# One decoder step on one core: the sampled tokens' state space steps move beside the recurrence heads, the gate norm's sums go through memory, the forget gate becomes a tangent

## The chip, the core and the metric

The kernel runs on one core of one Trainium2 chip. The metric is the device time in microseconds (us) of one execution. Its engines are PE (matrix products, with PEld for loading the stationary operand), DVE (vector), ACT (activations and copies), POOL (a second, slower vector engine) and SP (which here only issues transfers). Each engine works through its own list of instructions in order, so an instruction that waits holds up all that stand behind it on that engine.

## The reference, cut to what matters

One hybrid decoder layer is computed for a prompt of 1024 tokens and for 8 sampled tokens (one new token each, with their own stored states), which the kernel keeps side by side as 1032 columns.

```python
proj = rmsnorm(x, w['norm1_w']) @ w['w_in']
q_r, f_r, i_r, g_r, z, xbc_r, dt_r = jnp.split(proj, splits, axis=-1)
f = lb + (1.0 - lb) * sigmoid(f_r);  k = 1.0 - f;  q = silu(q_r)        # 8 heads, gated recurrence
o_a = rmsnorm(hgrn2_mix(q, k, i_r, log(f), S_h)) * silu(g_r)
xs, Bm, Cm = split(silu(causal_dwconv(xbc_r, buf_s)))                     # state space mixer, 2 groups
y, S_s_new = ssd_scan(X * dt, A * dt, Bh, Ch, S_s)
y = (y + D * X) * silu(z)
y = rmsnorm(y.reshape(Bsz, L, 2, 512)) * ssm_norm_w                       # norm over a group's 512 channels
x = x + concat(o_a, y) @ w['w_out']
x = x + (silu(causal_dwconv(gate)) * val) @ w['w_down']                   # gate, val = norm(x) @ w_up
```

For a sampled token the state space mixer is a single step: the stored state (64 x 128 per head) is scaled by its decay, a product of input and B is added, the new state is written out, and its product with C, summed over 128, is the output.

## The kernel before, in words

Channels lie on the 128 partitions and tokens along the free axis. A float32 product is made of three reduced ones (high and low parts of both operands), so a projection of 128 channels over 344 columns takes 24 matrix products; three such column chunks make a **job** of 72 steps (in_job). Jobs stand in one list: the state space inputs x0 to x7 with B and C, then the gate jobs z0 to z3, head 0's four jobs (f0, q0, v0, sg0), z4 to z7, and the jobs of heads 1 to 7, then the output projection. PE's list is written by hand: drive() runs a job's steps and, spread among them, the pieces of a second stream: the chunks of the state space scan (ssd_front, ssd_back), first for group 0 over the x jobs up to x7, then for group 1 over z0 to v0, and then head(h) over the jobs of head h + 1. after(n, work) puts a piece of work n steps later. On the other engines, and in SP's list of transfers, the framework orders the instructions by a plan of its own, at compile time.

What the change touches:

- **ssm_decode(g, i)** (L625): the sampled tokens' step for 128 channels, eight in all. For each half (4 tokens) it loads B and C of the tokens spread over the partitions (Bb, Cb) and the stored state (Sd); ACT scales the state (L638, 4 instructions), DVE multiplies B by the input (L639) and adds (L640), the state goes out, POOL multiplies by C (L642), DVE sums (L643). The steps of group 0 begin with jobs x5, x7, z0 and z1, beside the two scans; those of group 1 with z4 to z7.
- The scan: ssd_back needs the state S of the chunk before (DVE, L580) for its product yo, and ssd_front's xdt (DVE, L554) for yd. The convolution of a job (conv_tail, L347) puts three DVE instructions over 1056 columns into the same list.
- **ssm_gate(g)** (L653): each z job multiplies a tile of the scan's output by silu(z), and sums squares into gacc. For each of three chunks rstd() then sums over the partitions with a product by ones (ms), 344 columns wide on all 128 partitions, makes the reciprocal root in three DVE instructions (rstd_of, L649 to L651), and after the last one tail() scales four tiles (L694) and writes them to mix_d, with the sampled tokens' 8 columns in the same rows.
- **head_in(h)** (L806): f through Sigmoid (L818), q and sg through Silu. ACT keeps one table of functions at a time and loads another by an ACT_TABLE_LOAD.
- **head(h)** (L829): products named a (from k, v, f, q, scaled level by level on DVE, L872 and L873), od (the sampled tokens, from the state tiles Sh), ktp (transposes, copied to kt by ACT, L951), kv, the chain of states SS on DVE (L962, L964), and o. Sd and Sh use the same two buffers; Bb, Cb and vb the same four.

Of the kernel before, what the change touches and what calls it, by code (L numbers as in the profile page):

```python
# [50 lines left out]
def hybrid_layer(  # L51
# [37 lines left out]
    def bank(s, tag="mx"):  # L89
        return psmx.tile([P, 512], F32, tag=tag, bufs=NBANK[tag], name=nm(s))  # L90

    def mm(out, lhsT, rhs, start=True, stop=True):
        PE.matmul(out, lhsT, rhs, start=start, stop=stop)  # L93
# [55 lines left out]
    def col(name, i=0):  # L149
        c = vlay[name] + i  # L150
        return vcol[:, c:c + 1]
# [77 lines left out]
    def after(n, work):  # L229

        later.append([n, work])
# [123 lines left out]
    def xbc_evict(j, ext, c, cs, ps):  # L355
        e = min(cs.stop, T)
        A.copy(ext[:, 3 + cs.start:3 + e], ps[:, :e - cs.start])
        if c == 2:
            V.tensor_copy(ext[:, 3 + T:3 + T + 32].rearrange("p (b r) -> p b r", r=4)[:, :, 3:4],
                          ps[:, T - cs.start:].unsqueeze(2))  # L360
            V.tensor_copy(last11[:, j, :], ps[:, CH - 11:])

    def xbc_close(j, ext):
# [166 lines left out]
    def ssd_front(g, c, parts):  # L530
        tsl = slice(c * P, (c + 1) * P)
        hc = c * 16 + g * 8
        lm = []
        for q in range(2):
            csb = half("csb")
            csb3 = csb.rearrange("p (h l) -> p h l", l=P)
            h0 = hc + q * 4
            fetch(csb, cs_d[0, h0:h0 + 4, :].rearrange("h l -> (h l)").unsqueeze(0).to_broadcast([P, 512]))

            for h in range(4):  # L540
                A.activation(csb3[:, h, :], csb3[:, h, :], AF.Relu, scale=-1.0, bias=cst[:, h0 + h:h0 + h + 1])
            A.activation(csb, csb, AF.Exp, scale=-1.0)
            lm.append(csb3)
        bg = bank("bg")
        PE.transpose(bg[:, 0:P], BT[g][:, tsl], ident)
        mm(bg[:, P:2 * P], BT[g][:, tsl], CT[g][:, tsl])
        bt = small.tile([P, 2, P], F32, tag="bt", bufs=2, name=nm("bt"))
        A.copy(bt[:, 0, :], bg[:, 0:P])
        V.tensor_tensor(bt[:, 1, :], bg[:, P:2 * P], tri, op=ALU.mult)
        xp = bank("xp")  # L550
        for i in range(4):
            PE.transpose(xp[:, i * P:(i + 1) * P], Xg[g][i][:, tsl], ident)
        xdt, xde = half("xdt"), half("xde")
        V.tensor_tensor(h64(xdt), h64(xp), b64(dt, hc), op=ALU.mult)  # L554
# [70 lines left out]
    def ssm_decode(g, i):  # L625
        j = g * 4 + i
        xdd = small.tile([P, 2, ND], F32, tag="xdd", name=nm("xdd"))
        xdec = Xg[g][i][:, T:NT]
        V.tensor_tensor(xdd[:, 0, :], xdec, ddb[:, 0, j, :], op=ALU.mult)
        for b0 in (0, 4):  # L630
            bs = slice(b0, b0 + 4)
            Bb, Cb = tl("d", "Bb")[:, :512], tl("d", "Cb")[:, :512]
            for t_, r in ((Bb, 2 * g), (Cb, 2 * g + 1)):
                fetch(t_, bc_d[r, bs].rearrange("b n -> (b n)").unsqueeze(0).to_broadcast([P, 512]))
            Sd = tl("ld", "Sd")
            fetch(d4(Sd), state_ssm[0, bs, 2 * j:2 * j + 2].rearrange("b h p n -> (h p) b n"))
            for b in range(4):
                A.activation(d4(Sd)[:, b, :], d4(Sd)[:, b, :], AF.Copy, scale=ddb[:, 1, j, b0 + b:b0 + b + 1])  # L638
            V.tensor_tensor(d4(Bb), d4(Bb), cb(xdd[:, 0, bs]), op=ALU.mult)  # L639
            V.tensor_tensor(Sd, Sd, Bb, op=ALU.add)  # L640
            SP.dma_start(ssm_sample[0, bs, 2 * j:2 * j + 2].rearrange("b h p n -> (h p) b n"), d4(Sd))
            G.tensor_tensor(Cb, Sd, Cb, op=ALU.mult)  # L642
            V.tensor_reduce(xdd[:, 1, bs], d4(Cb), axis=mybir.AxisListType.X, op=ALU.add)  # L643
        V.scalar_tensor_tensor(xdec, xdec, d_bc[:, j:j + 1], xdd[:, 1, :], op0=ALU.mult, op1=ALU.add)

    def rstd_of(dst, tmp, ps, n):

        A.activation(dst, ps, AF.Abs_reciprocal_sqrt, bias=epsc, scale=1.0 / n)
        V.scalar_tensor_tensor(tmp, ps, n * EPS, dst, op0=ALU.add, op1=ALU.mult)  # L649
        V.scalar_tensor_tensor(tmp, tmp, -0.5 / n, dst, op0=ALU.mult, op1=ALU.mult)  # L650
        V.scalar_tensor_tensor(dst, tmp, 1.5, dst, op0=ALU.add, op1=ALU.mult)  # L651

    def ssm_gate(g):  # L653
        acc = []

        def z_job(i):
            j = g * 4 + i

            def begin():
                if i == 0:  # L660
                    acc.append(tl("g", "gacc"))
                if g:
                    ssm_decode(1, i)
                elif i < 2:
                    ssm_decode(0, i + 2)

            def evict(c, cs, ps):
                Y = Xg[g][i][:, cs]
                sz = tl("z", "sz")[:, :CH]
                A.activation(sz, ps, AF.Silu)  # L670
                V.tensor_tensor(Y, Y, sz, op=ALU.mult)
                if i == 0:
                    A.activation(acc[0][:, cs], Y, AF.Square)
                else:
                    A.activation(sz, Y, AF.Square)
                    (V if g or i == 3 else G).tensor_tensor(acc[0][:, cs], acc[0][:, cs], sz, op=ALU.add)
                if i == 3:
                    after(36 + 14 * g, lambda: rstd(c))
            in_job(f"z{j}", OFF_Z + j * P, evict, begin=begin)

        def rstd(c):
            cs = chunks[c]
            ps = bank("ms", "nx")
            mm(ps[:, :CH], ones, acc[0][:, cs])
            rstd_of(acc[0][:, cs], tl("z", "nt")[:, :CH], ps[:, :CH], 512)

            if c == NCH - 1:
                tail()

        def tail():  # L690
            for i in range(4):
                j = g * 4 + i
                Y = Xg[g][i][:, :NT]
                V.scalar_tensor_tensor(Y, Y, col("sn", j), acc[0][:, :NT], op0=ALU.mult, op1=ALU.mult)  # L694
                SP.dma_start(mix_d[8 + j], Y)

        for i in range(4):
            z_job(i)
# [35 lines left out]


    lbt = const.tile([P, 4, 8], F32, name="lbt")
    lo0, lo1 = vlay["lb"], vlay["lb"] + 8
    V.tensor_tensor(lbt[:, 0, :], vcol[:, lo0:lo0 + 8], vcol[:, lo1:lo1 + 8], op=ALU.max)
    V.tensor_tensor(lbt[:, 1, :], vcol[:, lo0:lo0 + 8], lbt[:, 0, :], op=ALU.subtract)
# [3 lines left out]
    V.reciprocal(lbt[:, 3, :], lbt[:, 3, :])  # L743
    V.tensor_tensor(lbt[:, 0, :], lbt[:, 1, :], lbt[:, 3, :], op=ALU.mult)
    V.tensor_scalar(lbt[:, 1, :], lbt[:, 0, :], -1.0, 1.0, op0=ALU.mult, op1=ALU.add)

    eye8 = const.tile([P, ND, ND], F32, name="eye8")
    G.memset(eye8, 1.0)
# [57 lines left out]
    def head_in(h):  # L806
        t = {}

        def f_end():
            f, k = t["f"], tl("big", "k")  # L810
            A.activation(f[:, :NT], f[:, :NT], AF.Identity, bias=lbt[:, 0, h:h + 1], scale=lbt[:, 1, h:h + 1])
            V.tensor_scalar(k[:, :NT], f[:, :NT], -1.0, 1.0, op0=ALU.mult, op1=ALU.add)
            t["k"] = k

        for n, off, func in (("f", OFF_F, AF.Sigmoid), ("q", OFF_Q, AF.Silu), ("v", OFF_I, AF.Copy),
                             ("sg", OFF_G, AF.Silu)):
            def evict(c, cs, ps, n=n, func=func):
                A.activation(t[n][:, cs], ps, func)  # L818
# [687 lines left out]
```

## Time and profile before

| | |
|---|---|
| median of 3 runs | 1765.32 us (1763.92 to 1766.82) |
| the profiled execution | 1763.89 us, its span 1762.2 us |
| PE busy | 1713.2 us, 97% of the span |
| DVE, ACT, POOL busy | 1105.4, 812.3, 482.0 us (63%, 46%, 27%) |
| granted PE clock, whole run | 0.994 |

PE is the engine to watch: what the others do matters where PE waits for them. A wait is shown as idle time before an instruction, with the engine and line that released it. PEclk is the clock that PE was granted in a stretch, 1.00 being full. Matrix products are pipelined: one lists as 0.32 us but the next starts 0.16 us later, so costs on PE are read from start to start.

### The profile page before, as it was taken

Reading aid. Unit: us, or ns where it says so; the run is one execution under the profiler, and the core shown is the slowest. Engines: PE = TensorE matmul, PEld = TensorE weight load, DVE = VectorE, ACT = ScalarE, POOL = GpSimd, SP = SyncE. Lnnn points to the kernel's source line nnn. Section 1 sums busy time; section 2 is a strip of 40 time slices with the busy share of each in tenths; the row PEclk is TensorE's granted clock in tenths of the full one; section 3 lists DMA queues with packets and bytes.
Section 4 is the critical chain, followed back from the end, with each engine's and each line's share of the span. In section 5 each row is a group of like instructions: output and inputs, shape, how many; then the busy total and the mean of one; then the engine's idle time right before and its main releaser. Section 6 shows DMA issues by size and latency. Waiting matters only on the chain. (4 is left out here: it accounts for less than half of the span.)

```text
span 1762.2 us, 38558 instructions
## 1 busy us (share of the span) xinstructions
PE 1713.2 (97%) x16111; PEld 1662.8 (94%) x16111; DVE 1105.4 (63%) x1988; ACT 812.3 (46%) x1450; POOL 482.0 (27%) x485
## 2 busy tenths in 40 slices
PE   7999899999999999999899999999999999999998
PEld 6999799998999999999799989999999999999997
DVE  6668966575554554466636688776667777445545
ACT  7577698454544454454423374334333434111114
POOL 2103332120110110112220355666666664000002
PEclk9999999999999999999899999999999999999999
DMA  5355744643321332234336742222222226422312
GB/s 166 68 147 155 189 117 136 179 139 105 88 89 51 98 87 80 69 115 143 110 113 212 245 127 73 73 85 85 85 73 73 80 78 217 152 85 78 98 61 97
DMA packets 249828, 199.17 MB, mean 113 GB/s; under 512 B 47212, under 2 KB 220822, under 8 KB 249638
## 3 DMA queue, kind: packets, MB, share of 16 engines
q1 hardware_dynamic: 249366, 196.61, 36.8%
q8 instruction: 126, 2.06, 0.5%
q14 instruction: 48, 0.39, 0.1%
q0 software_dynamic: 288, 0.10, 0.0%
HBM read 154.11 MB, written 46.94 MB: 114 GB/s over the span
## 5 line engine op out<-in xcount | busy, mean ns | idle before, releaser
L93 PE MATMUL mm<-hh,wh 128*128 128x344 f32 x1248 | 405.9, 326 | 2.0 <-issue 1.2
L93 PE MATMUL mm<-hl,wh 128*128 128x344 f32 x1248 | 405.5, 325 | 0.0
L93 PE MATMUL mm<-hh,wl 128*128 128x344 f32 x1248 | 402.4, 323 | 0.0
L93 PEld LDWEIGHTS mm<-hh,wh 128*128 128x128 f32 x1248 | 235.4, 189 | 6.5 <-issue 3.9
L93 PEld LDWEIGHTS mm<-hl,wh 128*128 128x128 f32 x1248 | 235.4, 189 | 4.5 <-issue 3.3
L93 PEld LDWEIGHTS mm<-hh,wl 128*128 128x128 f32 x1248 | 235.7, 189 | 1.8 <-issue 1.4
L190 ACT CAST wh<-ws 128x1024 fp32r<-128x1024 f32 x96 | 100.6, 1047 | 254.1 <-PE dn L93 135.0
L93 PE MATMUL ub<-uh,wh 128*128 128x258 f32 x704 | 199.3, 283 | 3.1 <-DVE fext L1319 2.7
L93 PE MATMUL ub<-ul,wh 128*128 128x258 f32 x704 | 199.0, 283 | 0.0
L93 PE MATMUL ub<-uh,wl 128*128 128x258 f32 x704 | 198.7, 282 | 0.0
L93 PE MATMUL dn<-ah,wh 128*128 128x256 f32 (+1 forms) x640 | 181.1, 283 | 2.0 <-DVE x L1436 2.0
L93 PE MATMUL dn<-al,wh 128*128 128x256 f32 (+1 forms) x640 | 180.6, 282 | 0.0
L93 PE MATMUL dn<-ah,wl 128*128 128x256 f32 (+1 forms) x640 | 180.1, 281 | 0.0
L192 DVE TENSOR_TENSOR wl<-ws,wh 128x1024 fp32r<-128x1024 f32 x88 | 108.7, 1235 | 75.7 <-ACT wh L190 68.6
L93 PE MATMUL mm<-mh,wh 128*128 128x258 f32 x512 | 148.2, 289 | 4.1 <-ACT x L1064 2.8
L93 PE MATMUL ua<-uh,wh 128*128 128x258 f32 x528 | 149.6, 283 | 1.3 <-DVE val L1331 1.3
L93 PE MATMUL ua<-ul,wh 128*128 128x258 f32 x528 | 149.3, 283 | 0.0
L93 PE MATMUL ua<-uh,wl 128*128 128x258 f32 x528 | 148.4, 281 | 0.0
L93 PE MATMUL mm<-ml,wh 128*128 128x258 f32 x512 | 146.9, 287 | 0.8 <-DVE ml L1024 0.8
L93 PE MATMUL mm<-mh,wl 128*128 128x258 f32 x512 | 146.5, 286 | 0.0
L93 PEld LDWEIGHTS ub<-uh,wh 128*128 128x128 f32 x704 | 132.9, 189 | 3.8 <-DVE fext L1319 2.9
L1269 DVE TENSOR_TENSOR wl<-wt,wh 128x512 fp32r<-128x512 f32 x88 | 89.6, 1037 | 74.2 <-ACT wh L1268 73.9
(351 smaller groups left out, 4037.2 us busy)
## 6 DMA issues: line engine op xcount, KB each, us to landing
ws<-in_w_in_dram SPq DMA_DIRECT2D x52, 512.0 KB
ws<-in_w_up_dram SPq DMA_DIRECT2D x44, 512.0 KB
ws<-in_w_out_dram SPq DMA_DIRECT2D x24, 512.0 KB
act_d<-val SPq DMA_DIRECT2D x22, 516.0 KB
al<-act_d SPq DMA_DIRECT2D x22, 516.0 KB
ws<-in_w_down_dram SPq DMA_DIRECT2D x22, 512.0 KB
ml<-mix_d SPq DMA_DIRECT2D x48, 172.0 KB
csb<-cs_d SPq DMA_DIRECT2D x32, 256.0 KB
```

Source lines behind the costliest of these rows:

```text
L93: PE.matmul(out, lhsT, rhs, start=start, stop=stop)
L190: A.copy(wh[:, :n], ws[:, :n])
L192: V.tensor_tensor(wl[:, :n], ws[:, :n], wh[:, :n].bitcast(F32), op=ALU.subtract)
L1269: V.tensor_tensor(lo[:, cs], sums[name], hi[:, cs].bitcast(F32), op=ALU.subtract)
```

## The change

- The eight ssm_decode steps leave the jobs x5, x7, z0, z1 and z4 to z7. They begin with jobs v and sg of heads 1 to 4, two to a head, so in the scan's stead they run beside head(0) to head(3). Their inputs and outputs move from the scan's tiles to a small tile of their own (xdk).
- After the fourth step of a group, decode_gate and decode_norm gate and normalise these 8 columns by themselves, with one small product by ones (dgs), and write them to mix_d.
- ssm_gate leaves the sampled columns out. rstd() runs once for a group: four products with 32 columns of ones put the sums of 1024 tokens on four strips of 32 partitions (256 columns each), one root over 256 columns follows, the result goes to memory (gr_d) and, 36 steps later, is read back spread over all partitions; 20 steps after that tail() scales the four tiles, 6 steps apart.
- f becomes Tanh of half the value, with the constants changed to match, since sigmoid(x) = 0.5 + 0.5 tanh(x / 2). Tanh is in the table that Silu is in.
- In ssd_front the second half's Relu comes ahead of both Exp. Head 0's k takes a buffer of another kind ("e").

```diff
         A.activation(acc[:, :T], acc[:, :T], AF.Silu)
-        A.activation(acc[:, T:NT], acc[:, T + 3:T + 32:4], AF.Silu)
+        A.activation(xdk[:, j, :] if j < 8 else acc[:, T:NT], acc[:, T + 3:T + 32:4], AF.Silu)
...
             ext.append(xbc_open())
-            if j in (5, 7):
-                ssm_decode(0, (5, 7).index(j))
...
             for h in range(4):
-                A.activation(csb3[:, h, :], csb3[:, h, :], AF.Relu, scale=-1.0, bias=cst[:, h0 + h:h0 + h + 1])
-            A.activation(csb, csb, AF.Exp, scale=-1.0)
+                held = A.activation(csb3[:, h, :], csb3[:, h, :], AF.Relu, scale=-1.0, bias=cst[:, h0 + h:h0 + h + 1])
             lm.append(csb3)
+        for csb3 in lm:
+            csb = csb3.rearrange("p h l -> p (h l)")
+            with tc.issue_after(held.ins):
+                A.activation(csb, csb, AF.Exp, scale=-1.0)
...
         V.scalar_tensor_tensor(xdec, xdec, d_bc[:, j:j + 1], xdd[:, 1, :], op0=ALU.mult, op1=ALU.add)
+        if i == 3:
+            after(110, lambda: decode_gate(g))
+
+    def decode_gate(g):
+        js = slice(4 * g, 4 * g + 4)
+        dg = small.tile([P, 6, ND], F32, tag="dg", bufs=1, name=nm("dg"))
+        V.tensor_tensor(xdk[:, js, :], xdk[:, js, :], szd[:, js, :], op=ALU.mult)
+        V.tensor_tensor(dg[:, 0:4, :], xdk[:, js, :], xdk[:, js, :], op=ALU.mult)
+        V.tensor_reduce(dg[:, 4, :], dg[:, 0:4, :].rearrange("p j b -> p b j"), axis=mybir.AxisListType.X, op=ALU.add)
+        after(30, lambda: decode_norm(g, js, dg))
+
+    def decode_norm(g, js, dg):
+        ps = bank("dgs", "nx")
+        mm(ps[:, :ND], ones, dg[:, 4, :])
+        rstd_of(dg[:, 4, :], dg[:, 5, :], ps[:, :ND], 512)
+        for j in range(js.start, js.stop):
+            V.scalar_tensor_tensor(xdk[:, j, :], xdk[:, j, :], col("sn", j), dg[:, 4, :], op0=ALU.mult, op1=ALU.mult)
+        SP.dma_start(mix_d[8 + js.start:8 + js.stop, :, T:NT].rearrange("j p b -> p j b"), xdk[:, js, :])
...
-                if g:
-                    ssm_decode(1, i)
-                elif i < 2:
-                    ssm_decode(0, i + 2)
...
-                if i == 3:
-                    after(36 + 14 * g, lambda: rstd(c))
+                if i == 3 and c == NCH - 1:
+                    after(36, rstd)
...
-        def rstd(c):
-            cs = chunks[c]
+        def rstd():
             ps = bank("ms", "nx")
-            mm(ps[:, :CH], ones, acc[0][:, cs])
-            rstd_of(acc[0][:, cs], tl("z", "nt")[:, :CH], ps[:, :CH], 512)
-
-            if c == NCH - 1:
-                tail()
+            for q in range(4):
+                mm(ps[32 * q:32 * q + 32, :256], ones[:, 0:32], acc[0][:, q * 256:(q + 1) * 256])
+            nt = tl("z", "nt")
+            rstd_of(nt[:, :256], tl("z", "nt")[:, :256], ps[:, :256], 512)
+            SP.dma_start(gr_d[g], nt[::32, :256])
+            after(36, rows)
+
+        def rows():
+            fetch(acc[0][:, :T], gr_d[g].rearrange("a t -> (a t)").unsqueeze(0).to_broadcast([P, T]))
+            after(20, lambda: spread(tail(), 6))
...
-        for n, off, func in (("f", OFF_F, AF.Sigmoid), ("q", OFF_Q, AF.Silu), ("v", OFF_I, AF.Copy),
+        for n, off, func in (("f", OFF_F, AF.Tanh), ("q", OFF_Q, AF.Silu), ("v", OFF_I, AF.Copy),
...
             def begin(n=n):
+                if 1 <= h <= 4 and n in ("v", "sg"):
+                    j = 2 * (h - 1) + (n == "sg")
+                    ssm_decode(j // 4, j % 4)
```

How the order of instructions moves, at three places. **DVE, beside group 0's scan at job x7**: the scan's S (a chunk's state), the convolution's xbc and, before, the decode step's sum xdd and product Bb. Before:

```order
L554 TENSOR_TENSOR xdt_2157<-xp_2152,dt 128x512
L643 TENSOR_REDUCE xdd_2317<-Cb_2320 128x4
L639 TENSOR_TENSOR Bb_2334<-Bb_2334,xdd_2317 128x512
L347 TENSOR_SCALAR xbc_2073<-ext_1903,vcol,xbc_2073 128x1056
L549 TENSOR_TENSOR bt_2149<-bg_2146,tri 128x128
L347 TENSOR_SCALAR xbc_2073<-ext_1903,vcol,xbc_2073 128x1056
L557 TENSOR_TENSOR csb_2132<-csb_2132,bt_2149 128x512
L347 TENSOR_SCALAR xbc_2073<-ext_1903,vcol,xbc_2073 128x1056
L557 TENSOR_TENSOR csb_2139<-csb_2139,bt_2149 128x512
L574 TENSOR_TENSOR ecs_2189<-yo_2192,ecs_2189 128x512
L580 TENSOR_TENSOR S_2200<-S_2200,st_2198 128x512
```

The same place now, with the lines of the changed kernel:

```order
L558 TENSOR_TENSOR xdt_2097<-xp_2092,dt 128x512
L347 TENSOR_SCALAR xbc_2046<-ext_1876,vcol,xbc_2046 128x1056 x3
L553 TENSOR_TENSOR bt_2089<-bg_2086,tri 128x128
L561 TENSOR_TENSOR csb_2072<-csb_2072,bt_2089 128x512
L561 TENSOR_TENSOR csb_2078<-csb_2078,bt_2089 128x512
L578 TENSOR_TENSOR ecs_2129<-yo_2132,ecs_2129 128x512
L584 TENSOR_TENSOR S_2140<-S_2140,st_2138 128x512
```

The two decode instructions between xdt and S are gone; the convolution's three still stand ahead of S. **DVE, in head 0**: group 1's tail (the four xbc<-xbc,vcol,gacc) and the levels of the head (f, q, k, v by tt). Before:

```order
L897 COPY_PREDICATED amc_4151<-mlow,a_598_4360 128x256
L694 TENSOR_SCALAR xbc_1671<-xbc_1671,vcol,gacc_3605 128x1032
L694 TENSOR_SCALAR xbc_1890<-xbc_1890,vcol,gacc_3605 128x1032
L694 TENSOR_SCALAR xbc_2073<-xbc_2073,vcol,gacc_3605 128x1032
L694 TENSOR_SCALAR xbc_2289<-xbc_2289,vcol,gacc_3605 128x1032
L812 TENSOR_SCALAR k_4343<-f_4166 128x1032
L192 TENSOR_TENSOR wl_4348<-ws_4346,wh_4347 128x1024
L872 TENSOR_TENSOR f_2999<-f_2999,tt_4150 128x128x4
L873 TENSOR_TENSOR q_3196<-q_3196,tt_4150 128x128x4
```

Now:

```order
L643 TENSOR_TENSOR Bb_4342<-Bb_4342,xdd_4325 128x512
L192 TENSOR_TENSOR wl_4074<-ws_4072,wh_4073 128x1024
L932 COPY_PREDICATED amc_3893<-mlow,a_536_4086 128x256
L722 TENSOR_SCALAR xbc_1677<-xbc_1677,vcol,gacc_3475 128x1024
L844 TENSOR_SCALAR k_4069<-f_3901 128x1032
L907 TENSOR_TENSOR f_2870<-f_2870,tt_3892 128x128x4
L908 TENSOR_TENSOR q_3058<-q_3058,tt_3892 128x128x4
```

One of the four tail instructions stands ahead of the head's f and q where four stood; the other three come after the next pair of levels. **ACT, in head 0**: am and kt are copies out of the head's products, v the projection's result, Sd the decode step's state. Before:

```order
L936 COPY am<-a_609_4602 64x8x64
L818 ACTIVATE v_4591<-mm_4592 128x344
L951 COPY kt_4675<-ktp_4676 128x512
L951 COPY kt_4682<-ktp_4683 128x512
L818 ACTIVATE v_4591<-mm_4661 128x344
```

Now:

```order
L971 COPY am<-a_554_4369 64x8x64
L850 ACTIVATE v_4358<-mm_4359 128x344
L642 ACTIVATE Sd_4331<-Sd_4331,ddb 128x128 x4
L642 ACTIVATE Sd_4346<-Sd_4346,ddb 128x128 x4
L986 COPY kt_4442<-ktp_4443 128x512
L986 COPY kt_4449<-ktp_4450 128x512
L850 ACTIVATE v_4358<-mm_4428 128x344
```

Eight scalings of a state that has yet to be loaded now stand ahead of the two copies kt.

More of the change, by code (lines that the diff above doesn't have):

```diff
@@ L661, in begin @@
                     acc.append(tl("g", "gacc"))
-                if g:
-                    ssm_decode(1, i)
-                elif i < 2:
-                    ssm_decode(0, i + 2)
             def evict(c, cs, ps):
+                cs = slice(cs.start, min(cs.stop, T))
+                n = cs.stop - cs.start
                 Y = Xg[g][i][:, cs]
@@ L670, in evict @@
                 A.activation(sz, ps, AF.Silu)
+                if c == NCH - 1:
+                    G.tensor_copy(szd[:, j, :], sz[:, n:])
+                sz = sz[:, :n]
                 V.tensor_tensor(Y, Y, sz, op=ALU.mult)
@@ L692, in tail @@
                 j = g * 4 + i
-                Y = Xg[g][i][:, :NT]
-                V.scalar_tensor_tensor(Y, Y, col("sn", j), acc[0][:, :NT], op0=ALU.mult, op1=ALU.mult)
-                SP.dma_start(mix_d[8 + j], Y)
+                Y = Xg[g][i][:, :T]
+                V.scalar_tensor_tensor(Y, Y, col("sn", j), acc[0][:, :T], op0=ALU.mult, op1=ALU.mult)
+                SP.dma_start(mix_d[8 + j][:, :T], Y)
+                yield
         for i in range(4):
@@ L745, in hybrid_layer @@
     V.tensor_scalar(lbt[:, 1, :], lbt[:, 0, :], -1.0, 1.0, op0=ALU.mult, op1=ALU.add)
+    V.tensor_scalar(lbt2[:, 0, :], lbt[:, 0, :], 0.5, 0.5, op0=ALU.mult, op1=ALU.add)
+    V.tensor_scalar(lbt2[:, 1, :], lbt[:, 1, :], 0.5, None, op0=ALU.mult)
     eye8 = const.tile([P, ND, ND], F32, name="eye8")
```

12 lines of the change are left out of this document (8 added, 4 removed).

## The prediction, as made before the changed kernel ran

> **What bounds the kernel now.** I read the page first: busy shares, then the clock row.
>
> ```profile
> span 1762.2 us, 38558 instructions
> PE 1713.2 (97%) x16111; PEld 1662.8 (94%) x16111; DVE 1105.4 (63%) x1988; ACT 812.3 (46%) x1450; POOL 482.0 (27%) x485
> PEclk9999999999999999999899999999999999999999
> ```
>
> PE is busy for 1713.2 of 1762.2 us, so a change pays only where PE waits, where its clock is halved, or where its own work shrinks; busy time saved on DVE or ACT by itself is worth nothing. The second view is the waits of PE between 120 and 440 us, the stretch in which the edited code runs (columns: us in total, times, longest).
>
> ```profile
> PE yo L93 <- DVE S L580: 3.1, 1, 3.1
> PE a L93 <- DVE q L873: 2.8, 1, 2.8
> PE ms L93 <- DVE vd L842: 1.4, 1, 1.4
> PE yd L93 <- DVE xdt L554: 1.4, 2, 1.0
> PE mm L93 <- ACT sz L670: 0.8, 1, 0.8
> PE xp L552 <- DVE S L580: 0.6, 2, 0.4
> PE a L93 <- DVE v L873: 0.5, 1, 0.5
> ```
>
> They total 10.6 us and come in three places. The third view is the windows: length, then busy time of PE, PEld, DVE, ACT and POOL, then the granted clock, DMA share, GB/s.
>
> ```profile
> 176.00:220.00 44.00, 38.92 (x262) 34.62 (x261) 42.25 (x68) 27.88 (x63) 15.02 (x12) 0.96 0.72 189
> 201.00:205.00 4.00, 0.86 (x7) 0.60 (x5) 4.00 (x7) 1.49 (x3) 0.13 (x1) 1.00 0.69 205
> 206.30:209.70 3.40, 3.40 (x19) 2.01 (x18) 3.40 (x8) 1.28 (x4) 1.31 (x1) 0.50 0.56 139
> 352.00:396.00 44.00, 41.81 (x379) 40.11 (x378) 31.21 (x54) 23.54 (x46) 10.11 (x8) 1.00 0.48 139
> 396.00:440.00 44.00, 40.72 (x553) 39.55 (x552) 25.65 (x45) 21.00 (x34) 0.00 (x0) 0.96 0.34 105
> 411.10:414.50 3.40, 3.40 (x63) 3.36 (x47) 2.84 (x5) 1.58 (x3) 0.00 (x0) 0.50 0.17 50
> 440.00:484.00 44.00, 44.00 (x694) 41.79 (x693) 25.74 (x46) 23.59 (x36) 5.40 (x4) 1.00 0.29 85
> ```
>
> In 176 to 220 us DVE is busy 42.25 of 44: there DVE, not PE, sets the pace (4.00 of 4.00 in 201 to 205, where PE has 0.86). In 396 to 440 DVE has room on average, so that wait is one of order. In 440 to 484, beside head 1, PE is at 44.00 of 44. And shortly after each of the two longest waits stand 3.40 us at a clock of 0.50.
>
> **The change, part by part.** The sum is made against the profiled execution's 1763.89 us (span 1762.2 and 1.7 around it), which lies 1.4 below the median of 1765.32; I add that at the end.
>
> *1. Decode steps out of group 0's scan.* The DVE groups of 176 to 220 us:
>
> ```profile
> L347 DVE SCALAR_TENSOR_TENSOR xbc<-ext,vcol,xbc 128x1056 f32<-128x1056 f32 x9 | 13.0, 1445 | 0.1
> L640 DVE TENSOR_TENSOR Sd<-Sd,Bb 128x512 f32<-128x512 f32 x4 | 3.7, 916 | 0.0
> L643 DVE TENSOR_REDUCE xdd<-Cb 128x4 f32<-128x512 f32 x4 | 2.7, 676 | 1.2 <-POOL Cb L642 1.2
> L639 DVE TENSOR_TENSOR Bb<-Bb,xdd 128x512 f32<-128x512 f32 x3 | 2.5, 839 | 0.0
> ```
>
> The last three go: 3.7 + 2.7 + 2.5 = 8.9 us of DVE's 42.25, and 1.2 of idling for POOL. The order before has one sum and one product of a decode step ahead of the convolution that delays S; they alone are 0.68 + 0.84 = 1.5 us, and the steps in front of them leave too. The waits of the scan are 3.1 + 1.4 + 0.6 = 5.1 us. With 8.9 us fewer in front, against 5.1 us of waiting, I let the 3.1 and the 1.4 go and keep 0.6, since the convolution's 13.0 us stay: **-4.5**. Bounds: 0 (S still stands behind the convolution) and -5.1.
>
> *2. The half clock after it.* 3.40 us at 0.50 hold 1.7 us of full-speed work: **-1.7** if the stretch goes with the wait, else 0.
>
> *3. One norm in place of three, 352 to 396 us.* Here the wait of ms for vd (1.4) goes: both use the same psum bank, and the one ms left stands 36 steps behind z7's last chunk. The wait of a projection for sz (0.8) is one for ACT, whose decode scalings at z4 to z7 leave: together -2.2, of which I count **-2.0**; bounds 0 and -2.2.
>
> *4. Tail in pieces, 396 to 440 us.*
>
> ```profile
> 401.65 4.90 DVE L694 SCALAR_TENSOR_TENSOR xbc<-xbc,vcol,gacc 128x1032 f32<-128x1032 f32 x4
> 408.21 0.69 DVE L872 TENSOR_TENSOR f<-f,tt 128x512 f32<-128x512 f32 x1
> ```
>
> Four tail instructions, 4.90 us in a row, stand ahead of head 0's f and q. Now one does (about 1.2 us), so f and q come up to 3.7 us sooner, and PE's waits for q and v are 2.8 + 0.5. One decode product is now queued there, at 0.84 us of the rows above, and 3.7 - 0.84 = 2.9 still covers the 2.8: I keep the 0.5, **-2.8**; bounds 0 and -3.3. *5. The half clock at 411.1 to 414.5:* **-1.7**, else 0.
>
> The norm's round trip through memory is new for these tiles; the nearest is that of a head's own norm:
>
> ```profile
> 446.25 0.56 SPq L997 DMA_DIRECT2D hr_d<-nt  x1
> 448.02 0.82 SPq L175 DMA_DIRECT2D sq<-hr_d  x2
> ```
>
> The fetch starts 1.8 us after the write. The edit puts 36 steps between the two and 20 behind the fetch; at 0.16 us a step or more from start to start these are 5.8 and 3.2 us, so the trip lies beside head 1's projections: cost 0 on PE. Were that cover gone, DVE would stand at the first tail instruction, with the head's levels behind it, for what is missing of 3.2 us, and a would wait as it did for q; 0 to 3.2 us, of which I take 0, as the trip's own rows are short.
>
> *6. PE's own work.*
>
> ```profile
> 267.04 0.74 PE L93 MATMUL ms<-gacc,ones 128*128 128x344 f32 x2
> 267.36 0.58 PE L93 MATMUL mm<-hh,wl 128*128 128x344 f32 x1
> 443.38 0.32 PE L93 MATMUL mm<-hh,wl 128*128 128x344 f32 x1
> 443.63 0.64 PE L93 MATMUL hms<-sq,ones 128*32 128x256 f32 x8
> 444.20 0.42 PE L93 MATMUL mm<-hh,wh 128*128 128x344 f32 x1
> L93 PE MATMUL dms<-od,ones 128*128 128x8 f32 x16 | 2.3, 216 | 0.0
> ```
>
> Plain float32 products list as two passes. An ms ends at 267.78 (its 0.74), from which the next product overlaps some 0.16: 0.58 each, six of them 3.5 us. The replacement has the shape of the heads' hms, from 443.63 to about 444.40: 0.77 for a group, two make 1.5; the two small products dgs have the shape of dms (0.216 a pass, two passes each): at most 0.9, I take 0.4. Net 3.5 - 1.9: **-1.6**; bounds -2.0 and -1.1.
>
> *7. What the steps meet beside the heads.* Nothing in 440 to 740 us waits on PE but this:
>
> ```profile
> PE mm L93 <- issue: 1.2, 1, 1.2
> L638 ACT ACTIVATE Sd<-Sd,ddb 128x128 f32<-128x128 f32 x64 | 20.9, 394 | 14.0 <-DMA Sd<-in_state_ssm_dram 7.8 <-DMA Cb<-bc_d 5.3 <-issue 0.9
> L642 POOL TENSOR_TENSOR Cb<-Sd,Cb 128x512 f32<-128x512 f32 x16 | 24.4, 1526 | 68.7 <-DVE Sd L640 55.3 <-DMA csb<-cs_d 9.0 <-DMA Cb<-bc_d 4.4
> 481.16 0.95 SPq L175 DMA_DIRECT2D Sh<-in_state_hgrn_dram  x2
> 484.23 0.69 DVE L853 TENSOR_TENSOR Sh<-Sh,f 128x512 f32<-128x512 f32 x1 [1.47 <-issue]
> 485.12 0.69 DVE L853 TENSOR_TENSOR Sh<-Sh,f 128x512 f32<-128x512 f32 x1 [0.20 <-DMA Sh<-in_state_hgrn_dram]
> 486.88 1.07 ACT L951 COPY kt<-ktp 128x512 f32<-128x512 f32 x2 [1.08 <-PE ktp L950]
> 490.41 1.95 PE L93 MATMUL kv<-vt,kt 128*128 128x128 f32 x16
> ```
>
> A decode step is 20.9 / 8 = 2.6 us of ACT, 24.4 / 8 = 3.0 of POOL and, from part 1's means, about 2 x (0.92 + 0.68 + 0.84) = 4.9 of DVE. In 440 to 484 DVE has 18 us free, ACT 20, POOL 39; a head gets two steps, so the sums fit. What is queued behind the new waits: on ACT, the eight scalings stand ahead of the kt copies, and PE's kv waits for kt. In head 1 kt ends at 487.95 and kv starts at 490.41, so 2.4 us of slack; the scalings' own 2.6 us go beside the transposes if the state has landed (the row shows 1.08 of idling before kt). On DVE, the Bb products stand ahead of head work. No row shows these places with a decode step; the bounds are 0, which is what the sums of free time give, and 8 us, four heads at 2.0 each (2.6 of scalings + 1.8 more of a late load, less the 2.4). I take **+1.5**, nearer the free-time row.
>
> *8. Table loads and tanh.*
>
> ```profile
> L818 ACT ACT_TABLE_LOAD x34 | 43.6, 1283 | 3.5 <-DMA mix_d<-xbc 2.1 <-PE mm L93 0.8
> ```
>
> Tanh lies in Silu's table, and the order has 81 loads where 99 stood: 18 x 1.283 = 23 us of ACT. ACT is at 46%, and PE waited for ACT only 0.8 us, counted in 3: 0, and cover for part 7. The swap of Relu and Exp and k's buffer likewise: 0, since PE shows no wait for either.
>
> **Sum:** -4.5 - 1.7 - 2.0 - 2.8 - 1.7 - 1.6 + 1.5 = -12.8, hence 1751.1 for a profiled run, and with the 1.4 above **1752.5** as a median.
>
> One rule speaks against terms 2 and 5. Rows: the waits of 3.1 us, and of 2.8 with 0.5, are each followed within 2 us by 3.40 us at 0.50, and neither the 1.4 nor the 0.8 at 352 to 396 is (clock 1.00 there). The Trainium skill (TensorE: Matmul & The Clock Gate, Part 1: The HAM clock gate) says that the clock halves after at least one idle window of about 3.4 us, free-running. By that rule none of these waits is long enough by itself, and the sum would be -9.4 instead of -12.8; by the rows the drop follows waits just shorter, so I keep both terms.
>
> **The rivals.**
>
> *B. S stays behind the convolution.* For it: L347 keeps 13.0 us in that window, and S is still listed behind two of its instructions. Against: 8.9 us leave. Terms 1 and 2 are lost: -12.8 + 6.2 = -6.6, 1758.7.
>
> *C. Slower: late states hold kt back.* The scalings stand in ACT's queue ahead of kt, and the state's load shares two buffers with Sh. Sh landed 3.1 and 4.0 us after its issue at 481.16; if the second Sd half starts that load only when Sh has freed its buffer, and lands over 2.4 us (kt's slack) later than the second Sh does now, kv waits. At 5.4 us later each of heads 1 to 4 waits 3.0, and, as after the 2.8 and 3.1 above, a stretch at half clock follows, 1.7: 4 x 4.7 = 18.8 in place of the 1.5, so -14.3 + 18.8: 1769.8. From 14.3 / 4 = 3.6 us a head on, the gains are used up. For it: ACT waited 7.8 us in all for Sd's loads. Against: its loads were issued well ahead in most cases, the DMA share beside head 1 is only 0.29, and 7.8 over eight steps is 1.0 each.
>
> *D. The cold stretches are not the waits' doing.* Both stay: -9.4, 1755.9. For it: the waits are a little shorter than the stretches. Against: both stretches stand right behind the two longest waits. It is the rule above as a mechanism of this kernel.
>
> *E. Gains eaten by the heads.* Each head with decode steps waits 3.0 us at DVE or ACT without the clock dropping: 12 in place of 1.5, 1763.0. That is the change not paying for itself: a wait moved rather than removed. For it: the levels' chain a to f to a on DVE is tight in head 0 (the 2.8 above). Against: 18 us of DVE are free beside head 1.
>
> **How the numbers follow.** Chances: forecast 0.58, B 0.14, D 0.08, E 0.09, C 0.11. About 0.2%, 3.5 us, is what a measurement of this kernel tells from no change. The forecast, B and D lie below 1761.8: faster 0.80; E within: 0.09; C slower: 0.11. The range goes from 1746 to 1762: the lower end has the forecast with terms 1, 3, 4 and 6 at their full bounds and part 7 at 0 (-15.8, 1749.5) and another 3.5 for the waits of the rest of the run that fewer ACT loads might take; the upper end takes in B and D, and the forecast with part 7 at its 8 (1759.0), and leaves out C and E, 0.2 together.
>
> **What would show it.** Step 1: in 176 to 220 us PE's waits for S at 0.6 or less and DVE clearly below 42 of 44; if B, a wait of some 3 us for S stays. Steps 2 and 5: a clock of 1.00 where 0.96 stands in both windows; if D, 0.96 without long waits. Step 3: no ms or mm wait in 352 to 396. Step 4: a for q under 0.5. Step 6: PE's count of 344-wide ms gone, hms-like groups in their place. Part 7: waits of kv for kt, or of a for f and q, in 440 to 740 under 2 us in all; C shows as kv waiting for kt with ACT idle for the Sd load before it, and a clock below 1.00 in those heads; E as waits without the clock. Part 8: 81 table loads and no change on PE by them. The prediction is wrong if PE waits at a place that shows none today: the most likely ones are beside heads 1 to 4.

## The result, and the profile after

| | before | changed |
|---|---|---|
| median | 1764.62 us (4 runs) | 1779.97 us (4 runs, 1778.48 to 1785.31) |
| ratio of the times | | 1.0085, 95% interval 1.0069 to 1.0101 |
| profiled execution: time, span | 1763.89, 1762.2 us | 1785.31, 1783.5 us |

The change makes the kernel about 15 us slower; a time of 1752.5 was forecast. The profiled execution is the slowest of the four, 5 us above the median, so the terms below are somewhat large for a middling run. Its page:

```profile
span 1783.5 us, 38586 instructions
PE 1714.5 (96%) x16119; PEld 1664.9 (93%) x16119; DVE 1097.6 (62%) x1998; ACT 784.3 (44%) x1430; POOL 484.5 (27%) x493
```

DVE and ACT are busy less than before, and the span is 21.3 us longer: the loss is waiting. The windows of the changed kernel (length, busy time of PE, PEld, DVE, ACT, POOL, granted clock, DMA share, GB/s) say where:

```profile
176.00:220.00 44.00, 44.00 (x311) 41.11 (x310) 31.46 (x52) 29.92 (x53) 7.53 (x8) 1.00 0.37 94
396.00:440.00 44.00, 44.00 (x463) 42.30 (x463) 28.01 (x53) 25.10 (x50) 5.13 (x4) 0.98 0.53 159
440.00:484.00 44.00, 36.75 (x628) 34.97 (x627) 25.23 (x44) 14.38 (x28) 6.02 (x4) 0.92 0.40 114
528.00:572.00 44.00, 34.96 (x508) 33.12 (x508) 20.20 (x46) 18.42 (x34) 4.57 (x4) 0.88 0.38 107
```

Beside group 0's scan (176 to 220) PE is now busy all the time, at full clock. Beside the heads (440 on), where it waited for almost nothing before, PE loses 7 to 9 us of 44. Its waits in 440 to 740 us (total, times, longest), which were one row of 1.2 us before:

```profile
PE dgs L93 <- DVE fbufT L334: 9.0, 1, 9.0
PE a L93 <- DVE q L908: 8.4, 3, 5.4
PE cst L333 <- DVE od L671: 4.6, 2, 3.2
PE mm L93 <- issue: 2.0, 1, 2.0
PE a L93 <- DVE amc L932: 1.0, 2, 0.7
```

These are 25.0 us. The clock adds to them: in the same 300 us stand four stretches at half clock, which the windows put around these times (the length comes first, then PE's busy time):

```profile
466.10:472.90 6.80, 5.36 (x141) 5.22 (x142) 6.29 (x11) 5.25 (x8) 0.00 (x0) 0.50 0.31 81
507.00:510.40 3.40, 3.40 (x18) 2.40 (x16) 1.22 (x2) 1.28 (x1) 0.00 (x0) 0.51 0.25 75
534.40:544.60 10.20, 3.81 (x14) 3.81 (x15) 5.87 (x17) 5.59 (x8) 0.00 (x0) 0.50 0.26 81
732.40:735.80 3.40, 3.40 (x14) 3.40 (x13) 1.22 (x1) 2.65 (x4) 0.00 (x0) 0.51 0.02 5
```

PE worked in them for 16.0 us in all (in the rest it was waiting anyway), and half of that, 8.0 us, is lost. So the heads cost 25.0 - 1.2 + 8.0 = 31.8, some 32 us. In 120 to 440 us the waits were 10.9 us before (the seven rows of the prediction and one of 0.3); now they are 4.9:

```profile
PE mm L93 <- issue: 2.0, 1, 2.0
PE yo L93 <- DVE S L584: 1.1, 1, 1.1
PE xp L556 <- DVE S L584: 1.0, 1, 1.0
PE yd L93 <- DVE xdt L558: 0.8, 2, 0.6
```

One half-clock stretch of the two there went as well, so the gain is 6.0 + 1.7 = 7.7; with the forecast's 1.6 for PE's own work, 31.8 - 9.3 = 22.5, near the 21.3 us between the spans. The sum isn't exact, and the last three rows are new: they stand in 264 to 352 us, beside group 1's scan, where before only the one of 0.3 stood.

What PE waits for is DVE, and DVE waits too. Its list around the longest wait, then SP's, then the rows of POOL and of PE:

```profile
527.73 1.21 DVE L913 TENSOR_TENSOR tt<-tt 128x16 f32<-128x16 f32 x2
535.55 0.69 DVE L643 TENSOR_TENSOR Bb<-Bb,xdd 128x512 f32<-128x512 f32 x1 [6.62 <-DMA Bb<-bc_d]
...
537.78 0.68 DVE L907 TENSOR_TENSOR f<-f,tt 128x512 f32<-128x512 f32 x1
...
540.52 0.22 DVE L334 COPY fbufT<-cst 128x64 f32<-128x64 f32 x1
```

```profile
527.28 3.22 SPq L890 DMA_DIRECT2D out_dram<-Sh  x2
530.54 1.42 SPq L175 DMA_DIRECT2D rt<-in_state_conv_ffn_dram  x1
532.01 0.42 SPq L175 DMA_DIRECT2D Bb<-bc_d  x1
```

```profile
524.51 1.04 POOL L887 TENSOR_TENSOR vb<-vb,k 128x512 f32<-128x512 f32 x1 [21.68 <-DMA vb<-vd_d]
...
528.78 1.30 POOL L889 TENSOR_TENSOR Sh<-Sh,vb 128x512 f32<-128x512 f32 x1
```

```profile
540.79 0.60 PE L93 MATMUL dgs<-dg,ones 128*128 128x8 f32 x2 [9.04 <-DVE fbufT L334]
```

Read from the bottom: dgs needs the one psum bank of its kind, which the copy fbufT has to empty. That copy stands in DVE's list behind the decode step's product Bb, and so do the head's levels f and q. Bb waits 6.6 us for its load. The load is issued at 532.01, behind the write of Sh in SP's list (two transfers, shown as one row, with a load rt after them), and the second of these writes can't go before POOL's addition ends at 530.08 (528.78 + 1.30). On the whole DVE waited 30.1 us at this line in 440 to 740 us; the trace puts half of that down to the load and names no releaser for the other half:

```profile
L643 DVE TENSOR_TENSOR Bb<-Bb,xdd 128x512 f32<-128x512 f32 x12 | 8.3, 688 | 30.1 <-DMA Bb<-bc_d 15.3 <-issue 14.7
```

### The profile page after: what moved, and what is told of

Same layout as the page of the kernel before. It is cut to its first block, busy times and chain, and to the rows that moved or that the text cites. A ratio compares the mean times of both kernels' runs of the same rounds, so it can differ in the third digit from the quotient of the medians.

```text
span 1783.5 us, 38586 instructions
## 1 busy us (share of the span) xinstructions
PE 1714.5 (96%) x16119; PEld 1664.9 (93%) x16119; DVE 1097.6 (62%) x1998; ACT 784.3 (44%) x1430; POOL 484.5 (27%) x493
```

## The experiments

Theory 1 was that one instruction, the product Bb in DVE's list, holds the head up because its load comes late, at first put down to the buffers of that load, which the head's vb would still hold. Theory 2 was crowding: that any decode work beside a head costs this much. Theory 3 blamed the norm's way through memory, or the tangent. Each kernel was timed against the kernel before on the same chip. Not all were on one chip, and the kernel before had medians from 1763.3 to 1765.2 us in these series, so differences of a microsecond or two between rows mean nothing by themselves.

| run | median us | ratio to before, 95% interval |
|---|---|---|
| e1, steps back at their old places | 1766.62 | 1.0012 (1.0001 to 1.0023) |
| e2, own buffers for B and C | 1780.45 | 1.0084 (1.0068 to 1.0099) |
| e3, one step per z job | 1763.89 | 0.9994 (0.9982 to 1.0006) |
| e4, Sigmoid | 1777.47 | 1.0069 (1.0049 to 1.0089) |
| e7, product on POOL | 1764.76 | 1.0006 (0.9996 to 1.0016) |
| e12, decode arithmetic behind the head's | 1754.71 | 0.9948 (0.9933 to 0.9962) |
| e13, that and the tail behind | 1752.22 | 0.9933 (0.9920 to 0.9945) |
| e15, one step per z job, tail behind | 1757.17 | 0.9965 (0.9953 to 0.9977) |
| e16, only the tail behind | 1774.41 | 1.0053 (1.0041 to 1.0065) |
| e18, as e2, write of Sh issued by POOL | 1772.81 | 1.0043 (1.0028 to 1.0057) |
| e19, as e13, Sigmoid | 1751.38 | 0.9921 (0.9907 to 0.9935) |
| e20, as e12, old norm | 1754.69 | 0.9941 (0.9921 to 0.9960) |

**e1, the steps back at their old places.**

```diff
+            if j in (5, 7):
+                ssm_decode(0, (5, 7).index(j))
...
-            after(110, lambda: decode_gate(g))
+            after(110 if g else 260, lambda: decode_gate(g))
...
+                if g:
+                    ssm_decode(1, i)
+                elif i < 2:
+                    ssm_decode(0, i + 2)
...
-                if 1 <= h <= 4 and n in ("v", "sg"):
-                    j = 2 * (h - 1) + (n == "sg")
-                    ssm_decode(j // 4, j % 4)
```

> The changed kernel with the eight decode steps begun where they began before (jobs x5, x7, z0, z1 and z4 to z7); the separate gate and norm of the 8 columns, the norm through memory, the tail in pieces and the tangent stay. Theory 1 (the loss of some 30 us beside heads 0 to 4 comes from the decode steps' product on DVE, which waits for loads into buffers that the head's vb still holds) and theory 2 (any decode work beside a head costs that, whatever its buffers): PE's waits in 440 to 740 us fall from 25 us to 2 or less, the scan's waits return (some 5 us), and the time is about 1757 (before less the terms 3 to 6 of the prediction, 8 us), ratio 0.995. Theory 3 (the norm through memory or the tangent holds the heads up): still above 1774, waits in 440 to 740 above 10 us.

The second edit only lets group 0's four steps end before they are gated. Beside the heads (440 to 740 us) the trace has no wait of PE at all, so theory 3 falls: it is the decode steps. Yet the time was 1766.6, not 1757. The scans' waits are back, 9.2 us where the kernel before had 5.1 (PE 39.37 of 44 at clock 0.96 in 176 to 220 us), and a wait for q stands where it stood before the change, longer than before. PE's wait, SP's fetch and DVE's list:

```profile
PE a L93 <- DVE q L911: 4.0, 1, 4.0
```

```profile
401.10 0.34 SPq L175 DMA_DIRECT2D gacc<-gr_d  x1
```

```profile
405.02 1.28 DVE L728 SCALAR_TENSOR_TENSOR xbc<-xbc,vcol,gacc 128x1024 f32<-128x1024 f32 x1 [2.80 <-DMA gacc<-gr_d]
...
410.19 0.69 DVE L910 TENSOR_TENSOR f<-f,tt 128x512 f32<-128x512 f32 x1
```

The norm comes back from memory 3.9 us after its fetch is issued; DVE stands at the first tail instruction until then, and the levels stand behind it. In the changed kernel DVE has the same wait ahead of 395.53, 3.30 us long, but there no product of PE waits for q.

**e2, own buffers.** From the third step on, B and C share one tile of the kind e, which the later heads leave free.

```diff
-            Bb, Cb = tl("d", "Bb")[:, :512], tl("d", "Cb")[:, :512]
+            if j >= 2:
+                bc = tl("e", "BC")
+                Bb, Cb = bc[:, :512], bc[:, 512:1024]
+            else:
+                Bb, Cb = tl("d", "Bb")[:, :512], tl("d", "Cb")[:, :512]
```

> The changed kernel, but from the third decode step on Bb and Cb take the two buffers of the kind e, which no head after head 0 uses, in place of those shared with vb; places and everything else as changed. Theory 1: the waits that DVE has at the product Bb go for these six steps, and with them the 9.0 us of dgs and the later of the waits for q and cst; those of the first two steps (about 8 to 11 us near 452 to 468, with clock) stay: 1764 to 1768, ratio about 1.000. Theory 2: within 5 us of the changed kernel, 1775 to 1783.

Nothing was gained: theory 1 as first put (the buffers are held) is wrong. DVE still waits for the loads (440 to 620 us), and SP's list shows what could be the reason, which e18 tests: the load stands behind the write of Sh whether its buffer is free or not.

```profile
DVE BC L647 <- DMA BC<-bc_d: 24.4, 7, 7.0
```

```profile
525.41 3.22 SPq L894 DMA_DIRECT2D out_dram<-Sh  x2
528.68 1.67 SPq L175 DMA_DIRECT2D rt<-in_state_conv_ffn_dram  x1
530.39 1.85 SPq L175 DMA_DIRECT2D BC<-bc_d  x4
```

**e3, one step with each of z0 to z7.** The call of ssm_decode(g, i) stands in z_job's begin.

> The changed kernel with the decode steps begun one with each of the jobs z0 to z7, so beside neither group 0's scan nor a head; buffers as changed. Theories 1 and 2: no waits beside the heads, none of 3 us for S: 1751 to 1757, ratio 0.992 to 0.996, if group 1's scan (beside z0 to z3) has room: DVE is busy there for about 26 of 44 us, and a step adds 5. Theory 3: above 1774.

The heads are free again (no wait of PE from 440 to 740 us), but the time is that of the kernel before: the scan has waits (2.9, 2.1 and 1.6 us), and a waits for q 5.3 us behind the tail. Missed by 7 us, for the same reason as e1.

**e4, Sigmoid in place of the tangent.**

```diff
-        for n, off, func in (("f", OFF_F, AF.Tanh), ("q", OFF_Q, AF.Silu), ("v", OFF_I, AF.Copy),
+        for n, off, func in (("f", OFF_F, AF.Sigmoid), ("q", OFF_Q, AF.Silu), ("v", OFF_I, AF.Copy),
...
```

The constants are set back to match (not shown).

> The changed kernel with Sigmoid in place of the tangent (18 or so ACT table loads of 1.28 us more). Theory 1 and 2: table loads lie beside other work except where od waits on ACT: 1780 to 1785, no gain. Theory 3 (tangent): falls by over 5 us.

1777.5, 2.5 us below the changed kernel, with intervals that overlap, though ACT loads tables 94 times where the changed kernel has 81: the tangent neither causes the loss nor pays here.

**e7, the product on POOL.**

```diff
-            V.tensor_tensor(d4(Bb), d4(Bb), cb(xdd[:, 0, bs]), op=ALU.mult)
+            G.tensor_tensor(d4(Bb), d4(Bb), cb(xdd[:, 0, bs]), op=ALU.mult)
```

> The changed kernel with one edit: the decode steps' product of B and the input is made by POOL instead of DVE. Own buffers for B and C did nothing, and the load of B stood in SP's list behind the write of Sh, which waits for POOL; so theory 1 now reads: DVE's list has the product ahead of the head's levels and of the small copies out of psum, the load is late, and whatever stands behind the product waits. Theory 1: with the product off DVE's list, PE's waits for q (8.4 us) and for dgs (9.0 us) beside the heads go, and some of the half clock; the wait of cst for od (4.6) stays: 1757 to 1765, ratio 0.996 to 1.001. Theory 2 (the sheer added work beside a head): 1776 to 1782.

One instruction on another engine takes 15 us off (14 by the ratios). PE's waits in 440 to 740 us are now:

```profile
PE cst L333 <- DVE od L671: 5.8, 2, 3.4
PE a L93 <- DVE q L908: 2.7, 1, 2.7
PE dgs L93 <- DVE fbufT L334: 2.0, 1, 2.0
```

17.4 us for q and dgs have become 4.7. What stays is cst, as expected; as the rows read, it needs the psum bank that holds dms until DVE has made od, and od stands behind the decode step's sums, which wait for POOL. In the changed kernel, DVE and PE:

```profile
502.86 0.69 DVE L647 TENSOR_REDUCE xdd<-Cb 128x4 f32<-128x512 f32 x1 [0.78 <-POOL Cb L646]
...
505.03 0.15 DVE L671 SCALAR_TENSOR_TENSOR od<-dms,od 128x8 f32<-128x8 f32 x1
```

```profile
505.24 0.42 PE L333 MATMUL cst<-ident,rt 16*128 16x16 f32 x4 [3.25 <-DVE od L671]
```

**e12, the decode arithmetic behind the head's.** Loads as changed, arithmetic 40 steps later (ACT's scalings, POOL's product and the gate and norm behind it too), and each of its DVE instructions ordered behind the head's newest level or od (mark):

```diff
+            mark[0] = V.tensor_tensor(qy[:, :, 1, :], qx[:, :, 1, :], ...
...
+        mark[0] = rstd_of(od[:, 1, :], od[:, 2, :], dps[:, :ND], P)
...
+        def rest():
+            for b0, bs, Bb, Cb, Sd in halves:
...
+                with tc.issue_after(mark[0].ins):
+                    V.tensor_tensor(d4(Bb), d4(Bb), cb(xdd[:, 0, bs]), op=ALU.mult)
...
+        after(40, rest)
```

> The changed kernel; the loads of a decode step are issued as before, but its arithmetic is written 40 steps later, and its DVE instructions are put behind the head's last level (for the step begun with v) or behind the head's od (for the step begun with sg). Nothing is left out, the same work lies beside the same heads. Theory 1: PE's waits between 440 and 740 us fall from 25 us to under 4 and the clock there is 1.00: 1752 to 1759, ratio 0.993 to 0.997. Theory 2: above 1772, since the work beside the heads is the same.

This decides between theories 1 and 2: the same instructions, beside the same heads, 25 us below the changed kernel. PE's waits in 440 to 740 us, and the group of the product, which now waits for nothing:

```profile
PE a L93 <- issue: 1.7, 1, 1.7
PE mm L93 <- issue: 1.3, 1, 1.3
PE cst L333 <- DVE od L681: 0.2, 1, 0.2
```

```profile
L649 DVE TENSOR_TENSOR Bb<-Bb,xdd 128x512 f32<-128x512 f32 x12 | 7.9, 682 | 0.0
```

And two of its windows, to be set beside those of the changed kernel:

```profile
440.00:484.00 44.00, 44.00 (x696) 42.28 (x695) 31.17 (x58) 17.23 (x38) 8.55 (x6) 1.00 0.56 159
528.00:572.00 44.00, 44.00 (x472) 41.79 (x471) 26.39 (x62) 24.41 (x48) 5.36 (x4) 1.00 0.49 136
```

DVE does more in them than before the change (31.17 against 25.74 in the first), and PE never waits. Head 0, ahead of these windows, has a wait that the changed kernel doesn't show: kv waits 1.5 us for kt, since ACT stands 3.5 us at the decode scalings for the load of Sd. e4, e7 and e18 have it too, with 1.0 to 1.4 us.

**e13, the tail behind the head's levels as well.**

```diff
-            after(20, lambda: spread(tail(), 6))
+            after(60, lambda: spread(tail(), 6))
...
+                with tc.issue_after((mark[0] if g else last_w[0]).ins):
+                    V.scalar_tensor_tensor(Y, Y, col("sn", j), acc[0][:, :T], op0=ALU.mult, op1=ALU.mult)
```

> As the run with the decode arithmetic behind the head's instructions, and with the four tail instructions of group 1 put behind the head's sixth level pair and begun 60 instead of 20 steps after the fetch from memory. If the wait of DVE for the fetched norm (3.3 us ahead of the levels near 393) is what keeps step 4 of the prediction from paying, this is 2 to 4 us below that run: 1749 to 1756. If not, the same within 1 us.

1752.2, 2.5 us below e12, as expected in size, though the intervals of the two ratios overlap. The wait of kv for kt is gone too, so the 2.5 isn't shown to be the tail's. This kernel beats both the kernel before and the changed one.

**e15, one step per z job with the tail behind.** The edits of e3 and of e13's tail.

> One decode step with each of the jobs z0 to z7, as in the earlier run of that kind (1763.9), and the tail instructions of group 1 put behind the head's levels, 60 steps after the fetch. If the 5.3 us for which head 0's products waited for q there came from the tail's wait for the fetched norm, they go with a stretch of half clock (1.7): 1756 to 1759, ratio 0.995. If it was the decode step of z7 itself: 1762 to 1765.

1757.2, 6.7 below e3 (5 by the ratios): the wait for q is gone from 352 to 440 us, so it was the tail's. The scan's waits remain.

**e16, only the tail behind.** The changed kernel with e13's tail edit alone.

> The changed kernel with the four tail instructions of group 1 alone put behind the head's sixth level pair, 60 steps after the fetch; the decode steps as changed. In the run where both were moved the tail's part was 2.5 us. Alone it should bring 1 to 4 us: 1776 to 1779; the decode waits stay (over 15 us between 440 and 740).

1774.4, 5.6 below the changed kernel, a little more than expected. DVE's wait for the norm is gone, but PE's in 352 to 440 us is what it was (2.2 us, 2.0 before this edit); what fell is the waits from 440 to 740, from 25.0 to 18.8 us. How the tail's place does that isn't shown. The decode waits stay.

**e18, as e2, with the write of Sh out of SP's list.**

```diff
-            SP.dma_start(hgrn_sample[0, bs, h].rearrange("b k v -> k b v"), d4(Sd))
+            G.dma_start(hgrn_sample[0, bs, h].rearrange("b k v -> k b v"), d4(Sd))
```

> The run with own buffers for B and C from the third decode step on (1780.5), with one more edit: the new state Sh of the heads is written out by a transfer that POOL issues behind its own addition, so the write leaves SP's list, in which B's load stood behind it. DVE's list still has the product ahead of the levels of heads 1 to 3. If the load was late because of that place in SP's list: DVE's waits at the product shrink from 24 us between 440 and 620 to under 8, PE's waits for dgs (8.7) and q (6.8) fall to under 5 in all, 1762 to 1770. If what makes the load late is something else (the loads rt that also stand ahead of it, or the load's own time of 3 to 5 us): over 1774.

The loads now go out at 517.50, 3.9 us behind the head's load of vb, instead of 530.39, 12.9 us behind it, and DVE's wait for them in 440 to 620 us is a quarter:

```profile
DVE BC L647 <- DMA BC<-bc_d: 6.0, 3, 2.6
```

```profile
523.10 3.06 DVE L647 TENSOR_TENSOR BC<-BC,xdd 128x512 f32<-128x512 f32 x2
```

```profile
517.50 1.87 SPq L175 DMA_DIRECT2D BC<-bc_d  x4
```

So the place in SP's list is what makes the load late. The time fell by 7.6 us, less than expected: dgs and q still wait 3.2 us each. The two products still stand ahead of the levels, and at this place they are 3.06 us long, where one takes 0.69 elsewhere; POOL is at work at the same time, which may be the reason. cst still waits 4.0.

**e19, as e13 with Sigmoid**, and **e20, as e12 with the old norm** (three sums of 344 columns, no way through memory).

> The run with decode arithmetic and tail behind the head's instructions (1752.2), with Sigmoid in place of the tangent. The prediction costed the tangent at 0, since ACT is at 45%: 1750 to 1755. If the table loads matter once nothing else holds PE up: 1756 or more.

> The run with the decode arithmetic behind the head's instructions (1754.7), but the norm of the 1024 prompt tokens as before: three sums of 344 columns on 128 partitions for a group, no way through memory, the four tail instructions in a row. Terms 3, 4, 5 and 6 of the prediction (8.1 us) say 1761 to 1764. If the norm's new form pays nothing by itself: 1753 to 1757.

e19 is 0.8 us below e13, inside the intervals: the tangent is worth nothing that can be measured, as costed. e20 equals e12 within the intervals, so nothing is seen of the 8.1 us of terms 3 to 6. It is no clean test: e20's executions lie between 1748 and 1760 us, and its trace has 4.0 us of waits beside head 1 that e12 doesn't have.

## Why the prediction was wrong, point by point

**The step that failed is part 7**, "what the steps meet beside the heads", taken at +1.5 us with 8 as its upper bound; it was some 32 in the profiled execution (25.0 - 1.2 of waits and 8.0 by the clock). The bound was made of sums of free time (DVE 18 us free, ACT 20) and of ACT's scalings ahead of kt. The sums were right: in e12 the same work fits beside the same heads, and PE waits 0.2 us for it from 440 to 740 us, and 1.5 in head 0. What was not priced is a wait in the middle of a list. The text named it ("on DVE, the Bb products stand ahead of head work") and then gave it no price of its own. To price it, one has to ask of the moved instruction not how long it is (0.69 us) but when its input arrives. The load stands in SP's list behind the write of Sh, that write behind POOL's addition, and that behind the trip of vd through memory: none of this is a resource that is full. The prediction asked what is queued behind the new waits on ACT and on DVE; it didn't ask what the new loads are queued behind in SP's list. Its last sentence did name the place, beside heads 1 to 4, where a wait was most likely to appear.

**Rival C had the sign and the kind, but the wrong place.** It had a late load hold up an in-order list, and the clock drop after each wait, 18.8 us in all; but it had ACT's scalings hold kt back. In the changed kernel kv waits for kt nowhere from 440 to 740 us. It was DVE, with the load of B and not that of the state. C's own wait exists, but only in head 0, 1.0 to 1.5 us in e4, e7, e12 and e18.

**Steps 1 and 2 held at their place.** PE is busy 44.00 of 44 at clock 1.00 in 176 to 220 us; e1 puts the steps back and has 39.37 at 0.96. But in the changed kernel 2.9 us of waits for S and xdt come up beside group 1's scan instead, so step 1's 4.5 was 2.2 on balance; e13, e19 and e20 don't have them. e12 and e20 are 8.6 and 10.4 us below the kernel before, against 6.2 forecast for these two steps; that most of it comes from them is likely, not shown.

**Steps 3 to 5 held in part.** The waits of ms for vd and of a projection for sz are gone in the changed kernel, as step 3 said. They are gone in e20 too, which has the old norm, and in e1, which has the steps at their old places: either half of the change takes them away, and the reason given isn't shown. Step 4's wait for q and v is gone as well. But the wait "mm <- issue" of 2.0 us stands near its place with a half-clock stretch behind it, so step 5's 1.7 was lost. And step 4 was right with little to spare: it counted on the tail being cut in pieces, one piece still stood ahead of the levels, and it waited 3.30 us for the norm, so that the working behind step 4, by which 36 and 20 steps cover the trip, was wrong twice: the 1.8 us in its rows run from the write to the issue of the fetch and leave out its landing (issued at 390.82, used at 395.53, 4.7 us more), and the order in which DVE meets the tail isn't set by the steps after which it was written (DVE was there 1.4 us after the fetch's issue, where 20 steps are 3.2). The text had the price of the missing cover (0 to 3.2 us) and took 0. In the changed kernel this wait of DVE didn't reach PE; in e1 and e3 it did, with 4.0 and 5.3 us for q, and e15 shows the latter by taking it away. Where the old norm's tail is kept, e20, the wait of 2.8 us for q is there as it was before.

**Step 6** measured about as forecast: a group's four products take 0.57 us, from 380.86 to 381.43, against the 0.77 taken; **step 8** at 0, by e4 and e19. A slip without weight: the bounds of the lower end of the range sum to -16.0, not -15.8.

With the decode arithmetic and the tail put behind the levels in DVE's list, e13, the time is 1752.2, that of the forecast. This is no confirmation of its sum but luck: e13 is another kernel than the one forecast, and what its gain is made of wasn't taken apart further. Left open is the wait "mm <- issue" of 2.0 us, at 393.39 and near 731, each with a half-clock stretch behind it; it has no releaser in the trace, stands in e12 and e13 with 1.2 to 1.8 us, and no run here tests it.

## What to carry to other kernels

Free time on an engine says whether moved work fits, not where it stands: for each moved instruction, find when its input lands, and what is queued behind it until then. Follow the load back through the list that issues it; a write that waits for a slow engine holds up every load behind it. Where the placing is left to a plan, an explicit order (this load early, this product behind that one) can be worth more than the move itself: here the second, in e12, turned +15 us into -9.

## What the runs showed of the hardware

The clock drops after short waits, if they fall badly. In the changed kernel a wait of 2.02 us was enough:

```profile
393.39 0.32 PE L93 MATMUL mm<-hh,wh 128*128 128x344 f32 x1 [2.02 <-issue]
```

```profile
394.60:397.80 3.20, 3.20 (x13) 3.20 (x12) 2.27 (x3) 0.00 (x0) 0.00 (x0) 0.50 0.51 155
```

After a longer one, of 2.69 us, in e7, the clock stayed at full speed. What decides can largely be read from the traces. Windows of 0.5 us put the starts of the five half-clock stretches at 394.41, 466.09, 507.05, 534.36 and 732.33 us, which are 21, 12, 8 and 58 times 3.413 us apart, and the stretches are one, two or three times 3.4 us long: the changes of the clock lie on a fixed grid of 3.41 us. Below are the window of that grid just ahead of the drop, and e7's two that share its wait:

```profile
391.00:394.41 3.41, 1.39 (x50) 1.46 (x37) 1.23 (x2) 1.25 (x1) 0.00 (x0) 1.00 0.66 177
```

```profile
447.49:450.91 3.42, 2.35 (x76) 1.86 (x74) 3.39 (x7) 1.60 (x3) 1.64 (x2) 1.00 0.60 202
450.91:454.32 3.41, 1.72 (x70) 1.71 (x71) 3.41 (x5) 0.00 (x0) 3.33 (x3) 1.00 0.30 84
```

PE was busy for 41% of the first, and for 69% and 50% of the other two. The 14 traces agree, from 120 to 1100 us: all 65 windows at full clock with PE busy for 47% or less were followed by half clock, and of those with 48 to 75% four were (53 to 56%) and 88 were not. So in these runs a wait costs clock when it takes about half of one window or more, and its length beyond that adds little work at half clock: 3.40 us after the 2.02, 5.36 after a wait of 5.42, 3.81 after the 9.04 of dgs. Several short waits can thus cost more than one long one of the same sum. The Trainium skill (TensorE: Matmul & The Clock Gate, Part 1: The HAM clock gate) has the clock halve after at least one idle window of about 3.4 us; the length of the half-clock stretches agrees with its window, the wait that sets one off does not, since a window half idle was enough, and here the measurement decides.
